# First two blocks' modulation columns by single-column matmuls, with the first x tile loaded first and the x tiles taken in turn

## The chip, the cores and the metric

The kernel runs on one core of one Trainium2 chip. The metric is the device time of one execution in microseconds (us); smaller is better. Engines are named as the profile names them: PE is TensorE (PEld its weight loads), DVE is VectorE, ACT is ScalarE, POOL is GpSimd, and SP is SyncE, whose queue issues all the transfers spoken of here.

## What is computed

A decoder layer on 2048 tokens of width 1024, cut to what the change touches:

```python
def hybrid_layer(x, c, positions, w_ada, b_ada, g_pre, w_in, ...):
    mod = jnp.einsum('bd,de->be', jax.nn.silu(c), w_ada) + b_ada
    shift, scale, gate = jnp.split(mod, 3, axis=-1)
    h = rmsnorm(x, g_pre) * (1.0 + scale[:, None, :]) + shift[:, None, :]
    proj = jnp.einsum('bsd,de->bse', h, w_in)
    gu, gv, gg, rq, rk, rv, rg = jnp.split(proj, PROJ_SPLITS, axis=-1)
    y_gmlp = gmlp_branch(gu, gv, gg, gmlp_ln_g, gmlp_ws, gmlp_bs)
    y_ret = retention_branch(rq, rk, rv, rg, positions, ret_gn_g)
    y = jnp.concatenate([y_gmlp, y_ret], axis=-1)
    y = rmsnorm(jnp.einsum('bsm,md->bsd', y, w_out), g_post)
    return x + gate[:, None, :] * y
```

## The kernel before

The 1024 channels are eight blocks of 128 (`kb` = 0 to 7). h is kept with the channels on the partitions, so scale and shift are one column each per block: `a_col[:, kb]` and `s_col[:, kb]`. Every large product is made of three f32r matmuls on high and low halves (`hh`, `hl` of h; `wh`, `wl` of the weights), 512 columns wide. The weights' halves are made on the way: `pump` takes the next weight block, ACT casts it to `wh` (L198), and another engine subtracts to get `wl` (L201).

The change lies in `start`, which handles the first 512 tokens (four tiles `xs[0]` to `xs[3]` of 128 tokens by 1024). For block 0 each tile goes through this chain:

- `stat(t)`: ACT squares and sums the tile (L283), POOL makes the reciprocal root of the mean in two operations (L286, L287);
- `scaled(t, a, b)`: DVE multiplies a range of the tile's columns by it (L933);
- `turn0(t)`: PE transposes the first 128 channels into PSUM (L922);
- `high0(t)`: ACT applies scale and shift and writes `hh` (L901); it needs `a_col` and `s_col` of block 0;
- `mms0(t)`: PE multiplies `hh` with the two weight halves (L929, L930).

`mod(kb)` makes the two columns of a block on DVE: for each it multiplies a slab of the modulation weights (`slab`, 128 by 1024, channels on the partitions) with `crow`, the row silu(c) spread to all partitions, and sums along the row (L897). `crow` is loaded ahead of all slabs and x tiles, and ACT applies silu to it (L879).

After the four tiles, `turn(1)` transposes block 1 of all four (L889), `qk_high(0)` makes two more products of block 0 (L977, L978), `h_low` on DVE makes `hl` of block 0 (L910, L912), and PE multiplies it (L1021, L1023). Then the loop over `kb` runs: in step `kb` PE multiplies block `kb` (L992, L993 and on) while ACT and DVE prepare block `kb + 1`: `hh` and `t` on ACT (both L901), `hl` on DVE (L912), then `mod(kb + 2)` on DVE and two `wl`. The stages after `start` (other tokens, rotary tables, retention, gMLP, the output product) are not touched.

What sets the order: on PE, ACT, DVE and POOL the instructions run in the order in which the program writes them, so an instruction that waits holds all that is written behind it on its engine. SP's queue issues transfers in its own order, and each waits until the buffer that it fills is free.

Of the kernel before, what the change touches and what calls it, by code (L numbers as in the profile page):

```python
# [11 lines left out]
F32 = mybir.dt.float32  # L12
# [3 lines left out]
AF = mybir.ActivationFunctionType  # L16
# [84 lines left out]
def tile_hybrid_layer(ctx: ExitStack, tc, x, xt, wm, wg, win, wun, wout, wst, cols, rows, pos, cst,  # L101
# [161 lines left out]
    def pump(eng=V, gap=1, ahead=3):  # L263
        if done[0] < len(worder):
            wsplit(worder[done[0]], eng, gap)
            done[0] += 1
        for i in worder[done[0]:done[0] + ahead]:
            wdma(i)
# [4 lines left out]
    def xload(pool, half, q, t, parts=1):  # L273
        row = half * HALF + q * QT + t * P
        xx = pool.tile([P, D], F32, name=f"xs{half}{q}{t}", tag="x", bufs=XBUF[half])
        for n in range(parts):
            cs = slice(n * D // parts, (n + 1) * D // parts)
            SP.dma_start(xx[:, cs], x[row:row + P, cs])
        return xx

    def xmean(xx, ss):
        jk = slot("jk", (xx.shape[-1],), BF16)
        S.activation(jk, xx, AF.Square, scale=1.0 / 32.0, accum_out=ss)  # L283
# [575 lines left out]
    def start(sp):  # L859
        def slab_load(kb):  # L860
            sl = [sp.tile([P, D], F32, name="slab", tag="x", bufs=XBUF[0]) for _ in range(2)]
            for t, n in zip(sl, range(2)):
                SP.dma_start(t, wm[kb, :, n, :])
            return sl

        crow = sp.tile([P, D], F32, name="crow")
        SP.dma_start(crow, rows[0:1, 2560:3584].partition_broadcast(P))
        slabs = {0: slab_load(0)}
        xs = [xload(sp, 0, 0, 0)]
        wdma(worder[0])  # L870
        xs += [xload(sp, 0, 0, t, 1 + t // 3) for t in range(1, QUAD)]
        wdma(worder[1])
        for n in (1, 2):
            slabs[n] = slab_load(n)
            for i in range(2):
                wdma(worder[2 * n + i])
        pv = [ps_m.tile([P, 512], F32, name=f"pv0{c}", tag="m") for c in range(QUAD)]
        pq0, pq1, tp = (ps_s.tile([P, 512], F32, name=n, tag="sm") for n in ("pq0", "pq1", "tp0"))
        S.activation(crow, crow, AF.Silu)  # L879
        xk, xn = {}, {}  # L880

        def xsums(tiles, ss, rs, ts):
            for t in ts:
                xmean(tiles[t], ss[:, t:t + 1])
                rsqrt_eps(rs[:, t:t + 1], ss[:, t:t + 1])

        def turn(kb):
            for c in range(QUAD):
                T.transpose(tp[:, c * P:(c + 1) * P], xs[c][:, kb * P:(kb + 1) * P], ident)  # L889
            xk[kb] = slot("xk")  # L890
            S.copy(xk[kb], tp)

        def mod(kb):
            for t, col, first, by in zip(slabs.pop(kb), (a_col, s_col), (b1g, cols_t[:, 8:16]),
                                         (cols_t[:, 24 + kb:25 + kb], 1.0)):
                jk = slot("jm", (D,), BF16)
                V.tensor_tensor_reduce(jk, t, crow, by, first[:, kb:kb + 1], ALU.mult, ALU.add,  # L897
                                       col[:, kb:kb + 1])

        def h_high(kb, src, hi):  # L900
            S.activation(hi, src, AF.Identity, bias=s_col[:, kb:kb + 1], scale=a_col[:, kb:kb + 1])  # L901

        def h_low(kb, parts, eng=V):
            hi, lo = hT[0, 0, kb]
            t = slot("t2")
            for cs, src in parts:
                if eng is S:
                    h_high(kb, src, t[:, cs])
                    continue
                V.tensor_scalar(t[:, cs], src, a_col[:, kb:kb + 1], s_col[:, kb:kb + 1], ALU.mult,  # L910
                                ALU.add)
            return lambda: V.tensor_tensor(lo, t, hi.bitcast(F32), ALU.subtract)  # L912

        ss = small.tile([P, QUAD + 1], F32, name="ss")
        rs = small.tile([P, QUAD], F32, name="rs")
        hi0 = hnew(0, 0, 0)[0]

        def t0(c):
            return (tp, pq1)[c % 2][:, c // 2 * P:(c // 2 + 1) * P]

        def turn0(c):
            T.transpose(t0(c), xs[c][:, 0:P], ident)  # L922

        def high0(c):
            h_high(0, t0(c), hi0[:, c * P:(c + 1) * P])

        def mms0(c):
            l, w = hchunk(0, c, 0), blocks[0]
            T.matmul(pv[c], l[0], w[0], start=True, stop=False)  # L929
            T.matmul(pv[c], l[0], w[1], start=False, stop=False)  # L930

        def scaled(t, a, b):
            V.tensor_scalar(xs[t][:, a:b], xs[t][:, a:b], rs[:, t:t + 1], None, ALU.mult)  # L933

        def stat(t):
            xmean(xs[t], ss[:, t:t + 1])
            rsqrt_eps(rs[:, t:t + 1], ss[:, t:t + 1])

        stat(0)
        pump(G, 0, 0)  # L940
        mod(0)
        scaled(0, 0, P)
        scaled(0, P, D)
        turn0(0)
        stat(1)
        high0(0)
        stat(2)
        scaled(1, 0, P)
        scaled(1, P, D)
        turn0(1)  # L950
        mms0(0)
        high0(1)
        xmean(xs[3][:, 0:512], ss[:, 3:4])
        scaled(2, 0, P)
        scaled(2, P, D)
        turn0(2)
        mms0(1)
        xmean(xs[3][:, 512:D], ss[:, 4:5])
        G.tensor_tensor(ss[:, 3:4], ss[:, 3:4], ss[:, 4:5], ALU.add)
        rsqrt_eps(rs[:, 3:4], ss[:, 3:4])  # L960
        high0(2)
        pump(G, 0, 0)
        scaled(3, 0, P)
        scaled(3, P, 2 * P)
        turn0(3)
        mms0(2)
        high0(3)
        mms0(3)
        low = h_low(0, [(slice(c * P, (c + 1) * P), t0(c)) for c in (0, 2, 1, 3)])
        low()  # L970
        mod(1)
        scaled(3, 2 * P, D)
        def qk_high(kb):
            w = blocks[KB + kb]
            for p, c in zip((pq0, pq1), range(2)):
                l = hchunk(0, c, kb)
                T.matmul(p, l[0], w[0], start=kb == 0, stop=False)  # L977
                T.matmul(p, l[0], w[1], start=False, stop=False)  # L978

        ss1 = small.tile([P, QUAD], F32, name="ss")  # L980
        rs1 = small.tile([P, QUAD], F32, name="rs")
        for kb in range(KB):
            f, e = kb == 0, kb == KB - 1
            if kb + 3 < KB:
                slabs[kb + 3] = slab_load(kb + 3)
                for i in range(2):
                    wdma(worder[2 * (kb + 3) + i])
            w, wq = blocks[kb], blocks[KB + kb]
            for c in range(QUAD):
                if not f:  # L990
                    l = hchunk(0, c, kb)
                    T.matmul(pv[c], l[0], w[0], start=False, stop=False)  # L992
                    T.matmul(pv[c], l[0], w[1], start=False, stop=False)  # L993
                if c == 1 and not e:
                    if kb == KB - 2:
                        xsums(xn, ss1, rs1, range(1))
                    turn(kb + 1)
                    pump(V, 0, 0)
                    pump(V, 0, 0)
            if f:  # L1000
                qk_high(kb)
            if not e:
                h_high(kb + 1, xk[kb + 1], hnew(0, 0, kb + 1)[0])
                low = h_low(kb + 1, [(slice(0, QT), xk[kb + 1])], S)
                low()
                if kb + 2 < KB:
                    mod(kb + 2)
            if kb == KB - 3:
                xn = [xload(sp, 0, 1, t) for t in range(QUAD)]
                SP.dma_start(wst_t, wst)  # L1010
                SP.dma_start(bs_b, rows[0:1, 0:512].rearrange("o (g t) -> o g t", g=4)
                             .partition_broadcast(P))
            if kb == KB - 2:
                G.tensor_tensor(wst_t, wst_t, mask.unsqueeze(1).broadcast_to([P, GROUPS, P]), ALU.mult)
                xsums(xn, ss1, rs1, range(1, 3))
            if e:
                xsums(xn, ss1, rs1, range(3, QUAD))
            if not f:
                qk_high(kb)
            for c in range(QUAD):  # L1020
                T.matmul(pv[c], hchunk(0, c, kb)[1], w[0], start=False, stop=e)  # L1021
            for p, c in zip((pq0, pq1), range(2)):
                T.matmul(p, hchunk(0, c, kb)[1], wq[0], start=False, stop=e)  # L1023
        return pv, (pq0, pq1), rs1
# [275 lines left out]
```

## Time and profile before

| | us |
|---|---|
| median of three runs | 882.3 (879.62 to 882.65) |
| the profiled execution's own time | 881.76 |
| its span in the trace | 880.0 |
| PE busy in the span | 845.7 |
| DVE busy | 673.3 |
| POOL busy | 358.1 |
| ACT busy | 313.0 |

The profiled execution lies 0.5 us under the median, and 1.76 us of its time lie outside the span. PE is busy for 96% of the span, so what is of interest are the stretches in which it is not, and they lie at the start (before the first block's matmuls run without a gap) and at the end. Times of single instructions are counted from the span's start.

### The profile page before, as it was taken

The page shows a single profiled execution, that of the slowest core. Times are in us where ns is not written, and L with a number is a line of the kernel's source. Part 1 is how long each engine was busy: PE and PEld are TensorE (multiplying, and loading weights), DVE is VectorE, ACT ScalarE, POOL GpSimd, SP SyncE. Part 2 cuts the span into 40 slices and gives each one's busy share as a digit, 9 for nine tenths or more (in the row PEclk, how much of TensorE's full clock was granted, in tenths as well). Part 3 has the DMA queues.
Part 4 walks back from the last instruction along what each step waited for, and adds up shares of the span by engine and source line. Part 5 has one row for each costly group of instructions (what it writes and reads, how often), then busy time and mean ns, then how long its engine had stood idle before and what let it go on. Part 6 is the DMA issues. An engine that isn't in the chain of part 4 may idle for free.

```text
span 880.0 us, 11841 instructions
## 1 busy us (share of the span) xinstructions
PE 845.7 (96%) x4074; PEld 696.3 (79%) x4074; DVE 673.3 (77%) x1275; ACT 313.0 (36%) x611; POOL 358.1 (41%) x403
## 2 busy tenths in 40 slices
PE   1999999999999999999999999999999999899996
PEld 0778888888888888888888888888888767688884
DVE  3989885665996768997786665897448898978885
ACT  4674223232363334431111221345343444333331
POOL 2031264345756236300443234675566000644551
PEclk9999999999999999999999999999999999999998
DMA  8971331310013424654222100011424854565422
GB/s 321 329 266 37 96 105 64 96 37 1 1 60 96 133 72 155 198 173 155 60 72 74 49 1 1 1 49 37 121 83 151 280 187 149 184 180 163 144 106 86
DMA packets 61884, 100.59 MB, mean 114 GB/s; under 512 B 5888, under 2 KB 22400, under 8 KB 61824
## 3 DMA queue, kind: packets, MB, share of 16 engines
q1 hardware_dynamic: 61824, 99.83, 34.6%
q8 instruction: 32, 0.52, 0.2%
q14 instruction: 28, 0.23, 0.1%
HBM read 83.03 MB, written 16.78 MB: 113 GB/s over the span
## 4 chain that ended last, share of the span: by engine, by line
PE 84%; DVE 6%; issue 3%; DMA 3%; ACT 2%; POOL 1%; SPq 0%; DVEq 0%; POOLq 0%; ACTq 0%
PE pqk L258 6%; PE pqk L256 6%; PE pqk L257 6%; PE pY L258 4%; PE pY L256 4%; PE pY L257 3%; PE pv L256 3%; PE pv L258 3%; PE pv L257 3%; PE prv L257 3%; PE prv L256 2%; PE pX L256 2%; PE prv L258 2%; PE pX L258 2%; PE pX L257 2%
## 5 line engine op out<-in xcount | busy, mean ns | idle before, releaser
L256 PE MATMUL pqk<-wh,hh 128*128 128x512 f32 x240 | 102.5, 427 | 0.0
L524 POOL TENSOR_TENSOR rA<-rA,rB 128x512 f32<-128x512 f32 x32 | 42.9, 1340 | 133.4 <-DVE rB L516 96.5
L258 PE MATMUL pqk<-wh,hl 128*128 128x512 f32 x240 | 94.7, 394 | 0.0
L257 PE MATMUL pqk<-wl,hh 128*128 128x512 f32 x240 | 93.8, 391 | 0.0
L538 ACT COPY qkT<-tp 128x512 f32<-128x512 f32 x32 | 18.8, 588 | 160.1 <-PE tp L529 160.1
L698 POOL TENSOR_SCALAR zrs<-zss 128x1 f32<-128x1 f32 x16 | 18.2, 1140 | 128.7 <-ACT jz L691 128.0
L201 DVE TENSOR_TENSOR wl<-wr,wh 128x512 fp32r<-128x512 f32 x62 | 63.0, 1030 | 0.2
L258 PEld LDWEIGHTS pqk<-wh,hl 128*128 128x128 f32 x240 | 45.0, 188 | 10.6
L256 PE MATMUL pv<-wh,hh 128*128 128x512 f32 x128 | 52.1, 407 | 0.0
L257 PEld LDWEIGHTS pqk<-wl,hh 128*128 128x128 f32 x240 | 45.5, 189 | 6.7 <-issue 0.2
L256 PEld LDWEIGHTS pqk<-wh,hh 128*128 128x128 f32 x240 | 45.4, 189 | 6.5 <-issue 0.2
L258 PE MATMUL pv<-wh,hl 128*128 128x512 f32 x128 | 50.1, 391 | 0.0
L257 PE MATMUL pv<-wl,hh 128*128 128x512 f32 x128 | 50.0, 390 | 0.0
L514 DVE TENSOR_TENSOR rA<-pqk,cos_t 128x512 f32<-128x512 f32 x28 | 19.3, 688 | 32.0 <-PE pqk L258 32.0
L201 DVE TENSOR_TENSOR wl<-ut,wh 128x512 fp32r<-128x512 f32 x48 | 42.9, 913 | 0.5 <-ACT wh L198 0.3
L582 DVE TENSOR_SCALAR yq<-o,gmv,grs 128x128 f32<-128x128 f32 x64 | 23.3, 405 | 23.9 <-POOL grs L575 23.9
L241 POOL TENSOR_TENSOR ut<-ur,ut 128x512 f32<-128x512 f32 x24 | 35.8, 1492 | 13.6 <-DVE yT L790 7.2
L461 ACT ACTIVATE vh<-pv,nbv,rsv 128x128 f32<-128x128 f32 x64 | 24.2, 457 | 47.4 <-POOL nbv L456 47.4
L256 PE MATMUL zY<-wh,yh 128*128 128x512 f32 x96 | 38.2, 398 | 2.2 <-DVE u L694 2.2
L198 ACT CAST wh<-ut 128x512 fp32r<-128x512 f32 x48 | 28.7, 621 | 31.7 <-POOL ut L241 31.7
L258 PE MATMUL zY<-wh,yl 128*128 128x512 f32 x96 | 38.3, 399 | 1.2 <-DVE yl L644 1.2
L790 POOL TENSOR_TENSOR yT<-yT,c 128x512 f32<-128x512 f32 x15 | 24.5, 1638 | 35.9 <-DVE c L810 25.8
(258 smaller groups left out, 2571.1 us busy)
## 6 DMA issues: line engine op xcount, KB each, us to landing
wr<-in_win SPq DMA_DIRECT2D x64, 256.0 KB, 3.9
ur<-in_wun SPq DMA_DIRECT2D x48, 256.0 KB, 3.5
slab<-in_wm SPq DMA_DIRECT2D x16, 512.0 KB, 6.2
ya<-yd SPq DMA_DIRECT2D x32, 256.0 KB, 3.8
xr<-in_x SPq DMA_DIRECT2D x16, 512.0 KB, 5.2
out<-xr SPq DMA_DIRECT2D x32, 256.0 KB, 2.8
or<-in_wout SPq DMA_DIRECT2D x28, 256.0 KB, 3.1
xt<-in_xt SPq DMA_DIRECT2D x24, 256.0 KB, 4.2
```

Source lines behind the costliest of these rows:

```text
L198: S.copy(hi, r)
L201: eng.tensor_tensor(lo, r, hi.bitcast(F32), ALU.subtract)
L241: G.tensor_tensor(r[name], r[a], r[b], ALU.subtract)
L256: T.matmul(ps, l[0], r[0], start=first, stop=False, skip_group_check=reopened)
L257: T.matmul(ps, l[0], r[1], start=False, stop=False, skip_group_check=reopened)
L258: T.matmul(ps, l[1], r[0], start=False, stop=last, skip_group_check=reopened)
L461: S.activation(vh[:, g, :], ps[:, g * P:(g + 1) * P], AF.Identity, bias=nb[:, g:g + 1], scale=rs[:, g:g + 1])
L514: V.tensor_tensor(A, ps.rearrange("p (g d) -> p g d", g=8), tab["cos"][:, ch, :].unsqueeze(1).broadcast_to([P, 8, 64]), ALU.mult)
L524: G.tensor_tensor(A, A, box["B"].rearrange("p g h d -> p (g h d)"), ALU.add)
L538: S.copy(qkT, box["tp"])
L582: V.tensor_scalar(yq[h][:, ch % QUAD, :], box["o"][:, i, :], mv[:, i, 0:1], rs[:, i:i + 1], ALU.subtract, ALU.mult)
L790: eng.tensor_tensor(y, y, by, ALU.mult)
```

## The change

Scale and shift of blocks 0 and 1 are made by `mod_pe` on PE, from slabs laid out with the contracted channels on the partitions (the host lays out these four slabs anew): eight f32 matmuls per column, each with 128x128 of the slab as the stationary operand and one column of silu(c), `sc`, as the moving one. Two small DVE operations then add the biases and the gain. `mod` on DVE stays for blocks 2 to 7. Since `crow` is then first needed for block 2, it is loaded later and its silu is moved into the loop. The first x tile is loaded ahead of all slabs. The statistics of the four x tiles are written in turn: a tile's statistics stand behind the `high0` of the tile before. The `wl` of the first two weight blocks move from POOL to DVE.

```diff
         crow = sp.tile([P, D], F32, name="crow")
+        xs = [xload(sp, 0, 0, 0)]
+        slabs = {0: slab_load(0)}
+        wdma(worder[0])
+        xs += [xload(sp, 0, 0, t) for t in range(1, QUAD)]
+        wdma(worder[1])
+        slabs[1] = slab_load(1)
+        for i in (2, 3):
+            wdma(worder[i])
         SP.dma_start(crow, rows[0:1, 2560:3584].partition_broadcast(P))
-        slabs = {0: slab_load(0)}
-        xs = [xload(sp, 0, 0, 0)]
-        wdma(worder[0])
-        xs += [xload(sp, 0, 0, t, 1 + t // 3) for t in range(1, QUAD)]
-        wdma(worder[1])
-        for n in (1, 2):
-            slabs[n] = slab_load(n)
-            for i in range(2):
-                wdma(worder[2 * n + i])
+        slabs[2] = slab_load(2)
+        for i in (4, 5):
+            wdma(worder[i])
...
+        pc = ps_s.tile([P, 512], F32, name="pc", tag="sm")
...
-        S.activation(crow, crow, AF.Silu)
...
+        def mod_pe(kb):
+            for n, t in enumerate(slabs.pop(kb)):
+                for k in range(KB):
+                    T.matmul(pc[:, 2 * kb + n:2 * kb + n + 1], t[:, k * P:(k + 1) * P], sc[:, k:k + 1],
+                             start=k == 0, stop=k == KB - 1)
+            V.scalar_tensor_tensor(a_col[:, kb:kb + 1], pc[:, 2 * kb:2 * kb + 1],
+                                   cols_t[:, 24 + kb:25 + kb], b1g[:, kb:kb + 1], ALU.mult, ALU.add)
+            V.tensor_tensor(s_col[:, kb:kb + 1], pc[:, 2 * kb + 1:2 * kb + 2],
+                            cols_t[:, 8 + kb:9 + kb], ALU.add)
...
         stat(0)
-        pump(G, 0, 0)
-        mod(0)
         scaled(0, 0, P)
+        mod_pe(0)
+        turn0(0)
+        pump(V, 0, 0)
         scaled(0, P, D)
-        turn0(0)
-        stat(1)
         high0(0)
-        stat(2)
...
+        for t in range(1, QUAD):
+            stat(t)
+            scaled(t, 0, P)
+            turn0(t)
+            high0(t)
+            mms0(t - 1)
+            scaled(t, P, D)
+        pump(V, 0, 0)
+        mms0(QUAD - 1)
         low = h_low(0, [(slice(c * P, (c + 1) * P), t0(c)) for c in (0, 2, 1, 3)])
         low()
-        mod(1)
-        scaled(3, 2 * P, D)
...
             if f:
                 qk_high(kb)
+                mod_pe(1)
             if not e:
                 h_high(kb + 1, xk[kb + 1], hnew(0, 0, kb + 1)[0])
                 low = h_low(kb + 1, [(slice(0, QT), xk[kb + 1])], S)
                 low()
+                if f:
+                    S.activation(crow, crow, AF.Silu)
```

On ACT at the start, before the change (`jk` rows are the statistics of a tile, `hh` rows are `high0`; `xs_104`, `108`, `110`, `112` are the four tiles):

```order
L879 ACTIVATE crow<-crow 128x1024
L283 ACTIVATE jk,ss<-xs_104 128x1024
L198 CAST wh<-wr 128x512
L283 ACTIVATE jk,ss<-xs_108 128x1024
L901 ACTIVATE hh<-tp_139,s_col,a_col 128x128
L283 ACTIVATE jk,ss<-xs_110 128x1024
L901 ACTIVATE hh<-pq_138,s_col,a_col 128x128
L283 ACTIVATE jk,ss<-xs_112 128x512 x2
L901 ACTIVATE hh<-tp_139,s_col,a_col 128x128
L198 CAST wh<-wr 128x512
L901 ACTIVATE hh<-pq_138,s_col,a_col 128x128
```

The same place on ACT after the change (the tiles are now `xs_99`, `107`, `109`, `111`):

```order
L283 ACTIVATE jk,ss<-xs_99 128x1024
L198 CAST wh<-wr 128x512
L913 ACTIVATE hh<-tp_138,s_col,a_col 128x128
L283 ACTIVATE jk,ss<-xs_107 128x1024
L913 ACTIVATE hh<-pq_137,s_col,a_col 128x128
L283 ACTIVATE jk,ss<-xs_109 128x1024
L913 ACTIVATE hh<-tp_138,s_col,a_col 128x128
L283 ACTIVATE jk,ss<-xs_111 128x1024
L913 ACTIVATE hh<-pq_137,s_col,a_col 128x128
L198 CAST wh<-wr 128x512
```

Before, the statistics of a tile stood ahead of the `hh` of the tile before; now they stand behind it.

On PE at the very start, before the change:

```order
L922 MATMUL tp_139<-cst_t,xs_104 128x128
L922 MATMUL pq_138<-cst_t,xs_108 128x128
L929 MATMUL pv_133<-wh,hh 128x512
L930 MATMUL pv_133<-wl,hh 128x512
L922 MATMUL tp_139<-cst_t,xs_110 128x128
```

The same place on PE after it (`pc` holds the columns in PSUM):

```order
L905 MATMUL pc<-sc,slab 128x1 x16
L934 MATMUL tp_138<-cst_t,xs_99 128x128
L934 MATMUL pq_137<-cst_t,xs_107 128x128
L941 MATMUL pv_132<-wh,hh 128x512
L942 MATMUL pv_132<-wl,hh 128x512
L934 MATMUL tp_138<-cst_t,xs_109 128x128
```

The sixteen single-column matmuls of block 0 now stand ahead of the first transpose.

On PE behind the fourth tile, before the change (`turn(1)`, `qk_high(0)`, then the products with `hl`):

```order
L889 MATMUL tp_139<-cst_t,xs_112 128x128
L977 MATMUL pq_137<-wh,hh 128x512
L978 MATMUL pq_137<-wl,hh 128x512
L977 MATMUL pq_138<-wh,hh 128x512
L978 MATMUL pq_138<-wl,hh 128x512
L1021 MATMUL pv_133<-wh,hl 128x512
```

The same place on PE after it:

```order
L891 MATMUL tp_138<-cst_t,xs_111 128x128
L974 MATMUL pq_136<-wh,hh 128x512
L975 MATMUL pq_136<-wl,hh 128x512
L974 MATMUL pq_137<-wh,hh 128x512
L975 MATMUL pq_137<-wl,hh 128x512
L905 MATMUL pc<-sc,slab 128x1 x16
L1021 MATMUL pv_132<-wh,hl 128x512
```

The sixteen single-column matmuls of block 1 now stand between `qk_high(0)` and the products with `hl`.

## Rows read from the trace of the kernel before

**Rows 1.** Page, parts 1 and 2: busy time by engine; granted clock in 40 slices

```profile
PE 845.7 (96%) x4074; PEld 696.3 (79%) x4074; DVE 673.3 (77%) x1275; ACT 313.0 (36%) x611; POOL 358.1 (41%) x403
PEclk9999999999999999999999999999999999999998
```

**Rows 2.** Stretches: length, busy PE, PEld, DVE, ACT, POOL, clock, DMA share, GB/s

```profile
26.79:60.00 33.21, 32.93 (x149) 25.47 (x150) 29.29 (x47) 23.74 (x39) 5.33 (x8) 1.00 0.92 319
60.00:200.00 140.00, 139.50 (x765) 117.74 (x764) 104.86 (x240) 43.48 (x88) 55.17 (x87) 1.00 0.23 73
```

**Rows 3.** Timeline of ACT: start, length, operation, [idle before, releaser]

```profile
6.68 1.06 ACT L879 ACTIVATE crow<-crow 128x1024 f32<-128x1024 f32 x1 [4.10 <-DMA crow<-in_rows]
11.10 1.06 ACT L283 ACTIVATE jk<-xs 128x1024 bf16<-128x1024 f32 x1 [3.36 <-DMA xs<-in_x]
...
15.05 0.46 ACT L901 ACTIVATE hh<-tp,s_col,a_col 128x128 fp32r<-128x128 f32 x1 [0.86 <-PE tp L922]
15.41 1.04 ACT L283 ACTIVATE jk<-xs 128x1024 bf16<-128x1024 f32 x1
...
18.35 0.46 ACT L901 ACTIVATE hh<-tp,s_col,a_col 128x128 fp32r<-128x128 f32 x1
18.71 0.61 ACT L198 CAST wh<-wr 128x512 fp32r<-128x512 f32 x1
21.40 0.46 ACT L901 ACTIVATE hh<-pq,s_col,a_col 128x128 fp32r<-128x128 f32 x1 [2.08 <-PE pq L922]
...
25.92 0.82 ACT L901 ACTIVATE hh<-xk,s_col,a_col 128x512 fp32r<-128x512 f32 x1 [0.28 <-DVE s_col L897]
```

**Rows 4.** Timeline of POOL, behind the third tile's statistics

```profile
16.91 0.55 POOL L287 TENSOR_TENSOR rs<-rs,nhalf 128x1 f32<-128x1 f32 x1
```

**Rows 5.** Timeline of DVE, first 29 us

```profile
3.52 0.16 DVE L130 SCALAR_TENSOR_TENSOR b1g<-cols_t 128x8 f32<-128x8 f32 x1
8.71 1.34 DVE L897 CUSTOM_DVE_ANT_0 jm<-slab,crow,b1g 128x1024 bf16<-128x1024 f32 x1 [5.03 <-DMA slab<-in_wm]
...
9.97 1.28 DVE L897 CUSTOM_DVE_ANT_0 jm<-slab,crow,cols_t 128x1024 bf16<-128x1024 f32 x1
...
17.49 0.88 DVE L933 TENSOR_SCALAR xs<-xs,rs 128x128 f32<-128x128 f32 x2 [0.81 <-POOL rs L287]
...
20.95 0.72 DVE L910 TENSOR_SCALAR t<-tp,a_col,s_col 128x128 f32<-128x128 f32 x2
...
26.27 1.29 DVE L201 TENSOR_TENSOR wl<-wr,wh 128x512 fp32r<-128x512 f32 x2
27.48 0.69 DVE L912 TENSOR_TENSOR hl<-t,hh 128x512 fp32r<-128x512 f32 x1
28.09 1.34 DVE L897 CUSTOM_DVE_ANT_0 jm<-slab,crow,b1g 128x1024 bf16<-128x1024 f32 x1
```

**Rows 6.** Timeline of PE: third tile's transpose, block 1's transposes, `qk_high(0)`, first `hl` products

```profile
17.84 0.48 PE L922 MATMUL tp<-cst_t,xs 128*128 128x128 f32 x1 [0.36 <-DVE xs L933]
...
22.93 1.04 PE L889 MATMUL tp<-cst_t,xs 128*128 128x128 f32 x4
23.64 0.56 PE L977 MATMUL pq<-wh,hh 128*128 128x512 f32 x1
...
24.74 1.08 PE L1021 MATMUL pv<-wh,hl 128*128 128x512 f32 x4
```

**Rows 7.** Timeline of PE's weight loads at the start

```profile
16.42 0.33 PEld L930 LDWEIGHTS pv<-wl,hh 128*128 128x128 f32 x1
...
22.93 0.65 PEld L889 LDWEIGHTS tp<-cst_t,xs 128*128 128x128 f32 x3 [0.20 <-issue]
```

**Rows 8.** Groups by shape, matmuls, then weight loads, of L467: count, busy us, mean ns

```profile
L467 PE MATMUL mx<-wst_t,vh 128*128 128x128 f32 x128 | 16.8, 274 | 0.0
...
L467 PEld LDWEIGHTS mx<-wst_t,vh 128*128 128x128 f32 x128 | 16.7, 191 | 1.3
```

**Rows 9.** Timeline of PE, one chunk's L467 matmuls in the full flow

```profile
214.05 1.05 PE L467 MATMUL mx<-wst_t,vh 128*128 128x128 f32 x8
```

More of the change, by code (lines that the diff above doesn't have):

```diff
@@ L939, in start @@
         stat(0)
-        pump(G, 0, 0)
-        mod(0)
         scaled(0, 0, P)
+        mod_pe(0)
+        turn0(0)
+        pump(V, 0, 0)
         scaled(0, P, D)
-        turn0(0)
-        stat(1)
         high0(0)
-        stat(2)
[L948 to L968, printed above, removed]
+        for t in range(1, QUAD):
[7 more added lines that the diff above has]
+        mms0(QUAD - 1)
         low = h_low(0, [(slice(c * P, (c + 1) * P), t0(c)) for c in (0, 2, 1, 3)])
         low()
-        mod(1)
-        scaled(3, 2 * P, D)
         def qk_high(kb):
@@ L1254 @@
     wm = np.stack([wa[1], wa[0]], axis=2)
+    for kb in range(2):
+        for n in range(2):
+            wm[kb, :, n, :] = w_ada[:, (1 - n) * D + kb * P:(1 - n) * D + (kb + 1) * P].reshape(
+                KB, P, P).transpose(1, 0, 2).reshape(P, D)
     wg = w_ada[:, 2 * D:].reshape(KB, P, D)
```

## The prediction

> **What bounds the kernel now.** I read the page first: PE is busy 845.7 of 880.0 us [rows 1], so 34.3 us are left. The stretches say where they are not: from 26.79 to 60 PE is busy 32.93 of 33.21 us, from 60 to 200 it is busy 139.50 of 140 [rows 2]. More than half of the gap lies at the start: the statistics of the first tile begin at 11.10, and its `hh`, without which PE has no product, at 15.05 [rows 3]. Everything behind the start runs on PE without slack, so I take a shift of the point where block 1's flow begins to the end one for one. That point I measure by ACT's `hh` of block 1, at 25.92 [rows 3]; PE's first product of block 1 follows it.
>
> How 25.92 comes about, by ACT's timeline: x tile 0 has landed at 11.10, behind `crow` (6.68) and the slabs. Of the four `high0` the first begins at 15.05, the third at 18.35 and the last at 21.40 [rows 3], 6.35 after the first. From there to 25.92 are 4.52 us, and `hh` of block 1 waited for `s_col` from DVE [rows 3], which is `mod(1)`.
>
> **First term: the four tiles in turn.** The order rows show each tile's statistics behind the `hh` of the tile before. The trace has this very loop once: `hh` of tile 0 at 15.05, right behind it the squares of tile 2 at 15.41, POOL's power at 16.91 [rows 4], DVE's scaling at 17.49 [rows 5], PE's transpose at 17.84 [rows 6], `hh` of tile 2 at 18.35 [rows 3]. That is 3.30 us, each step starting when the one before ends. Before, two such loops ran interleaved; now there is one. Three rounds make 9.90 us from the first to the last `high0`, against 6.35: +3.55. PE at its higher clock would save some 0.2 in a round, which I leave to the range. The tile order takes something away from this: the later tiles land earlier than before by one 512 KB transfer (`crow`, behind them now), but they have landed long before ACT asks.
>
> **Second term: when the first `high0` can start.** It needs the transpose of tile 0 and both columns of block 0. Tile 0 takes `crow`'s place in the queue, so it lands at about 6.68 [rows 3] in place of 11.10. That gain of 4.4 us is worth nothing if the columns are later. The slabs keep their places behind one 512 KB transfer: the first has landed at 8.71, the second by 9.97, where DVE read it without a wait [rows 5]. Behind them, `mod` took DVE two operations. Now PE runs sixteen f32 matmuls, and the trace says what one f32 matmul is: L467 is called 64 times (16 chunks of four groups) and has 128 records with 128 weight loads [rows 8]. So a call is two passes, each with a load of its own, and a `mod_pe` is 32 passes.
>
> The price of a pass with one moving column stands nowhere in the trace; a weight load for it does. Eight passes of L467 take 1.05 us with the last one 0.27 [rows 8, 9], so (1.05 - 0.27) / 7 = 0.11 us from pass to pass in the full flow, load included. At the start PE is slower: there a load takes 0.33 us [rows 7] against 0.19 [rows 8], and three loads in a row take 0.65, 0.22 each [rows 7]. The granted clock is printed as full in those slices [rows 1], so I go by the durations and call the two levels 1.2 and 2.4 GHz. Bounds for a pass: 0 below (all of it might hide), 0.33 above (loads that don't overlap at the lower level). PE has done nothing before 8.71, so I take the lower level for all of block 0, at twice 0.11, 0.21: 32 x 0.21 = 6.7, which ends at 15.4. The last pass's own tail (0.2) and two small DVE operations like L130's 0.16 [rows 5] add 0.55: the first `high0` starts at 16.0, against 15.05: +0.95. The transpose of tile 0 stands behind the 32 passes on PE and is ready at about 15.9, so it hides.
>
> The Trainium skill, "TensorE: Matmul & The Clock Gate", section "LDWEIGHTS (loading the stationary operand)", gives a load of 128 columns as 128 / 1.2 ns, 107 ns, with no second figure for another clock. The 0.11 of the full flow agrees; the longer loads of rows 7 speak against one figure for both levels. By it the time is that of the second rival below.
>
> With both terms the last `high0` starts at 16.0 + 9.9 = 25.9, against 21.40: +4.5.
>
> **Third term: from the last `high0` to block 1.** Before, 4.52 us. Now, in order: `hh`'s share 0.36 (18.35 to 18.71 [rows 3]), the cast 0.61 [rows 3], its `wl`, which has moved from POOL to DVE ahead of the reads of the transposes, 0.65 (half of 1.29 [rows 5]), those reads of the first bank 0.72 [rows 5]: 2.4 with the hops. Only then may `turn(1)` overwrite that bank: 1.04 [rows 6]. `qk_high(0)` takes 1.10 (23.64 to 24.74 [rows 6]): 4.55. Then the 32 passes of block 1; PE has worked without pause by then and I take 0.11: 3.5. With 0.55 for the tail and DVE, `hh` of block 1 starts 8.6 us behind the last `high0`: +4.1. `mod(1)`, 2.6 us of DVE, is saved, but it no longer ends last. The slabs of block 1 come one transfer earlier than before and wait for PE by then.
>
> **Fourth term: `crow`.** Its silu (1.06 [rows 3]) now stands behind block 1's second activation on ACT, and `mod(2)` waits for it. Before, `mod(2)` started 0.61 behind the start of `hl` (27.48 to 28.09 [rows 5]), which itself started as that activation ended. So it starts 1.06 behind it now, +0.45, and the loop carries that on.
>
> POOL loses two subtractions and one add, which nobody waits for. The DVE work for the small columns is in the sums. The later slabs wait for PE's reads in place of DVE's: the slabs whose buffers `mod_pe(1)` frees are for blocks 3 and 4, which DVE comes to only after `mod(2)`, so they hide as before; if not, the loop would pay a landing once.
>
> **Sum.** 0.95 + 3.55 + 4.1 + 0.45 = 9.05 us. On the profiled execution's 881.76 that is **890.8 us**; the median of the runs lies 0.5 above that execution, which is within the noise of the sum.
>
> **Rivals.** *Cheap passes, no slower than before.* If a single-column pass cost nothing, the first `high0` would start at 9.97 + 0.55 = 10.5, the last at 20.4, `hh` of block 1 at 20.4 + 4.55 + 0.55 = 25.5 against 25.92, and with `crow` the time is 881.8: a tie. Each 0.01 us of a pass adds 0.48 (the second slab's 16 and block 1's 32; the first slab's hide behind the second's landing), so up to about 0.09 the change stays inside 0.5%. For it: only one column moves. Against it: every pass has its own load [rows 8]. The time at half that bound is 884.0. The Trainium skill, "TensorE: Matmul & The Clock Gate", section "Wait — 56ns, not 53.3ns?", gives 25 ns as the least distance between matmuls however small; by that the sum would be 1.2 us over the tie.
>
> *Loads at 0.11 from the start.* If the level doesn't matter to a load, or PE rises to the higher one during block 0's passes, these end at 8.71 + 3.5 = 12.2, the first `high0` starts at 12.8, and the sum is 3.2 less: 887.6. For it: 32 passes in a row keep PE at work. Against it: the 0.33 and 0.22 of rows 7.
>
> *PE stays at the lower level.* If columns of width one don't hold the higher clock, block 1's passes take 0.21 too, +3.2, and the first products of block 1 start slow, as `qk_high`'s first did (0.56 [rows 6]); some 1.5 us more. That gives 895.5. With loads that don't overlap at either level (0.33, then 0.19) it is 32 x 0.12 + 32 x 0.08 = 6.4 over the sum: 897.2.
>
> **How the numbers follow.** Forecast, about 890.8: 0.50. Loads at 0.11 throughout, 887.6: 0.20. Lower level kept, 895.5: 0.12, and loads that don't overlap, 897.2: 0.04. Cheap passes, 881.8 to 886: 0.14. The range reaches from 885.5, inside the cheap case, to 897, and leaves out some 0.16. A measurement tells about 0.5% from no change, 877.9 to 886.7. Slower by more: 0.50 + 0.12 + 0.04 and most of the 0.20, 0.83. Within it: 0.15. Faster: 0.02, since even passes for nothing only tie; it would take slabs that land some 5 us earlier.
>
> **What would show it.** Right: `high0` at about 16, 19.3, 22.6 and 25.9, with ACT idle between each tile's statistics and its `hh`; 64 weight loads for `pc`, the first ones 0.2 apart and the later ones 0.11; `hh` of block 1 near 34.5; from there on the same flow as before, 9 us later. Wrong: rounds clearly under 3.3, loads under 0.1 apart in block 0, or `hh` of block 1 before 30.

## The result, and the profile after

The changed kernel takes 894.66 us (median of four executions, 890.29 to 897.16) against 882.17 us (879.62 to 882.65): a ratio of 1.0142, with a 95% interval of 1.0097 to 1.0187. It is slower by 12.5 us, where 9 were forecast. The profiled execution took 893.83 us. Its page, with the span, the busy time of each engine and the granted clock in 40 slices, answers to [rows 1]:

```profile
span 892.1 us, 11959 instructions
...
PE 859.9 (96%) x4138; PEld 711.6 (80%) x4138; DVE 669.9 (75%) x1272; ACT 311.4 (35%) x609; POOL 355.1 (40%) x400
...
PEclk9999999999999999999999999999999999999998
```

The span has grown by 12.1 us, PE's busy time by 14.2, and what PE doesn't work has shrunk from 34.3 to 32.2. ACT, DVE and POOL have less to do than before. The balance doesn't say by itself where the time went: block 0's passes count as busy time of PE, and they stand where PE waited before. The timelines do. Behind the start PE has still no slack (stretches in the columns of [rows 2]; the first ends where `hh` of block 1 is about to start):

```profile
26.79:36.00 9.21, 8.56 (x37) 7.86 (x36) 3.54 (x8) 1.62 (x3) 0.00 (x0) 1.00 0.14 42
36.00:60.00 24.00, 24.00 (x102) 19.78 (x103) 17.93 (x30) 14.73 (x23) 0.00 (x0) 1.00 0.72 241
60.00:200.00 140.00, 139.53 (x752) 117.13 (x752) 108.00 (x235) 51.45 (x101) 53.00 (x81) 1.00 0.33 103
```

In the first stretch PE is busy 8.56 of 9.21 us while ACT works 1.62, so ACT waits for PE. ACT's timeline shows it row by row (start, length, operation, idle before it and what ended it), as [rows 3] did before:

```profile
5.42 1.06 ACT L283 ACTIVATE jk<-xs 128x1024 bf16<-128x1024 f32 x1 [2.73 <-DMA xs<-in_x]
...
15.48 0.46 ACT L913 ACTIVATE hh<-tp,s_col,a_col 128x128 fp32r<-128x128 f32 x1 [4.95 <-DVE s_col L909]
15.84 1.05 ACT L283 ACTIVATE jk<-xs 128x1024 bf16<-128x1024 f32 x1
18.79 0.46 ACT L913 ACTIVATE hh<-pq,s_col,a_col 128x128 fp32r<-128x128 f32 x1 [1.81 <-PE pq L934]
...
22.08 0.46 ACT L913 ACTIVATE hh<-tp,s_col,a_col 128x128 fp32r<-128x128 f32 x1 [1.80 <-PE tp L934]
...
25.37 0.46 ACT L913 ACTIVATE hh<-pq,s_col,a_col 128x128 fp32r<-128x128 f32 x1 [1.80 <-PE pq L934]
...
37.62 0.81 ACT L913 ACTIVATE hh<-xk,s_col,a_col 128x512 fp32r<-128x512 f32 x1 [7.08 <-DVE s_col L909]
...
42.56 0.59 ACT L893 COPY xk<-tp 128x512 f32<-128x512 f32 x1 [2.48 <-PE tp L891]
43.05 1.15 ACT L198 CAST wh<-wr 128x512 fp32r<-128x512 f32 x2
44.09 0.81 ACT L913 ACTIVATE hh<-xk,s_col,a_col 128x512 fp32r<-128x512 f32 x1
```

Three places stand out. The first `high0` waits 4.95 us for the columns although tile 0 has been there since 5.42. Each later `high0` waits 1.8 us for its tile's own transpose. And `hh` of block 1, at 37.62, waits 7.08 us for `s_col`; before, it stood at 25.92 and waited 0.28.

PE's timeline has what they wait for (`pc` are the passes of `mod_pe`, L974 and L975 `qk_high(0)`, L1021 the products with `hl`, L990 those of block 1):

```profile
8.10 6.96 PE L905 MATMUL pc<-sc,slab 128*128 128x1 f32 x32 [8.10 <-DMA slab<-in_wm]
...
18.27 0.47 PE L934 MATMUL pq<-cst_t,xs 128*128 128x128 f32 x1 [2.90 <-DVE xs L945]
...
27.76 1.11 PE L891 MATMUL tp<-cst_t,xs 128*128 128x128 f32 x4 [0.65 <-DVE t L922]
28.53 0.78 PE L974 MATMUL pq<-wh,hh 128*128 128x512 f32 x1
...
29.95 0.63 PE L975 MATMUL pq<-wl,hh 128*128 128x512 f32 x1
30.38 6.82 PE L905 MATMUL pc<-sc,slab 128*128 128x1 f32 x32
37.06 2.05 PE L1021 MATMUL pv<-wh,hl 128*128 128x512 f32 x4
...
42.75 0.55 PE L990 MATMUL pv<-wl,hh 128*128 128x512 f32 x1
43.14 0.40 PE L989 MATMUL pv<-wh,hh 128*128 128x512 f32 x1
```

A `mod_pe` is 32 passes, as forecast, and takes 6.96 us for block 0 and 6.82 for block 1. With a last pass of 0.35 that is (6.96 - 0.35) / 31 = 0.21 us from pass to pass, in both. The same lower level shows in the products: 0.63 a product at 29.95, 2.05 for four at 37.06 (1.08 before [rows 6]), and only from 43.14 on the 0.40 of the full flow. By the durations PE runs at the lower level from its first instruction to some 43 us, with pauses of 2.90, 1.96, 1.96 and 0.65 us up to 27.76 and none after that. The printed clock is 1.00 all the way in this trace, so here the durations tell and not that column.

The chain of work that ended last, in its first 48 us, has both groups of passes whole, each in one piece:

```profile
8.10 6.97 PE pc L905 x32
...
30.58 6.62 PE pc L905 x32
```

### The profile page after: what moved, and what is told of

Same layout as the page of the kernel before. It is cut to its first block, busy times and chain, and to the rows that moved or that the text cites. A ratio compares the mean times of both kernels' runs of the same rounds, so it can differ in the third digit from the quotient of the medians.

```text
span 892.1 us, 11959 instructions
## 1 busy us (share of the span) xinstructions
PE 859.9 (96%) x4138; PEld 711.6 (80%) x4138; DVE 669.9 (75%) x1272; ACT 311.4 (35%) x609; POOL 355.1 (40%) x400
## 4 chain that ended last, share of the span: by engine, by line
PE 88%; DVE 5%; DMA 3%; issue 2%; ACT 1%; POOL 1%; SPq 0%; DVEq 0%; POOLq 0%; ACTq 0%
PE pqk L258 6%; PE pqk L256 6%; PE pqk L257 6%; PE pY L258 3%; PE pY L256 3%; PE pY L257 3%; PE pv L258 3%; PE pv L256 3%; PE pv L257 3%; PE prv L257 2%; PE prv L256 2%; PE prv L258 2%; PE pX L257 2%; PE pX L258 2%; PE pX L256 2%; PE pZ L257 2%
## 5 line engine op out<-in xcount | busy, mean ns | idle before, releaser
L201 DVE TENSOR_TENSOR wl<-wr,wh 128x512 fp32r<-128x512 f32 x64 | 65.4, 1034 | 3.1 <-ACT wh L198 3.0
L198 ACT CAST wh<-wr 128x512 fp32r<-128x512 f32 x64 | 37.4, 617 | 5.3 <-DMA wr<-in_win 5.3
```

Of the source, the lines that this page charges most:

```text
L198: S.copy(hi, r)
L201: eng.tensor_tensor(lo, r, hi.bitcast(F32), ALU.subtract)
```

## The experiments

The theory: three separate costs stand one behind the other on the way to block 2: the tiles in turn, block 1's passes on PE, and a PE that stays at the lower level. The rivals: that one of them explains all of it, that a pass hides behind something else, or that the lower level is an accident of the start that work on PE cures. Each kernel below ran beside the kernel before (median 881.9 for the first four, 881.71 for the others, 882.17 beside the changed kernel); differences between two of them can be off by that 0.5 us.

| kernel | first `high0` | last `high0` | `hh` block 1 | `hh` block 2 | median against before, us |
|---|---|---|---|---|---|
| before | 15.05 | 21.40 | 25.92 | 30.74 | 0 |
| after | 15.48 | 25.37 | 37.62 | 44.09 | +12.5 |
| block 1's columns on DVE | 15.61 | 26.45 | 32.71 | 37.52 | +7.8 |
| statistics one tile ahead | 15.58 | 20.74 | 32.98 | 39.45 | +7.1 |
| PE kept busy at the start | 13.54 | 23.44 | 35.68 | 40.99 | +10.2 |
| block 0's passes twice | 22.67 | 32.56 | 44.81 | 51.28 | +18.6 |
| before, tiles in turn | 14.79 | 24.69 | 30.12 | 34.93 | +5.6 |
| before, x tile first | 14.63 | 21.01 | 25.53 | 30.34 | -1.6 |
| all three cures | 12.79 | 18.47 | 24.73 | 29.54 | -0.9 |
| two cures, PE not kept busy | 15.50 | 20.66 | 26.93 | 31.74 | +1.1 |

The middle columns are starts in us on ACT's timeline of the profiled execution. The shift at block 2 is what comes out at the end, within 2 us either way, in every line. So a shift of the start does go to the end one for one, as the prediction took it. Most of what is left between the traces has a cause that they show. In five of them (before, block 1's columns on DVE, PE kept busy, x tile first, all three cures) the granted clock falls near 770 us to the lower level for 3.4 us; in the other five it does not. From `hh` of block 2 to the end the five with the fall take 849.2 to 850.5 us, the five without it 848.0 to 848.8. The same place before and after (columns of [rows 2]):

```profile
764.50:768.00 3.50, 3.50 (x10) 2.76 (x9) 2.89 (x5) 0.00 (x0) 0.00 (x0) 0.51 1.02 375
```
```profile
776.50:780.00 3.50, 2.68 (x12) 2.24 (x13) 3.50 (x6) 0.40 (x1) 1.28 (x1) 1.00 1.00 382
```

Twelve 512-wide products there take 4.41 us before (from 763.72) and 2.83 after (from 777.32), and in both PE had waited 2.17 us just ahead of them. Why the level fell in one and not in the other stays open; the change doesn't touch this stage.

### Block 1's columns back on DVE

```diff
+        SP.dma_start(crow, rows[0:1, 2560:3584].partition_broadcast(P))
         slabs[1] = slab_load(1)
...
-        SP.dma_start(crow, rows[0:1, 2560:3584].partition_broadcast(P))
...
             scaled(t, P, D)
+            if t == 2:
+                S.activation(crow, crow, AF.Silu)
...
         low()
+        mod(1)
...
                 qk_high(kb)
-                mod_pe(1)
...
-                if f:
-                    S.activation(crow, crow, AF.Silu)
```

The host lays out only the slabs of block 0 anew here.

> The changed kernel with the columns of block 1 back on DVE (mod(1), with crow loaded ahead of block 1's slabs and its silu on ACT between the third and fourth tile). Theory, that block 1's 32 passes on PE at the lower clock level stand on the path: hh of block 1 starts some 5 us behind the last high0 in place of 12.25, PE rises to the higher level about 6 us sooner, and the time falls by 7 to 8.5 us, to about 886.5. Rival, that the time went into the tiles' turns and the columns of block 0 alone, and block 1's wait only shows a delay that something else would have caused (the loads, or DVE): the time falls by under 2 us.

Measured: 889.74 us (ratio 1.0088, 1.0073 to 1.0103), 4.9 under the changed kernel, 6.6 at block 2. That is less than the 7 to 8.5 that were expected, and far more than the rival's 2. Of the 6.6 some 1.6 are lost near 770 us, where this trace has the fall of the clock and that of the changed kernel has not. From this kernel's timeline ACT's rows around the last `high0`, then PE's first products with `hl`:

```profile
22.56 1.05 ACT L966 ACTIVATE crow<-crow 128x1024 f32<-128x1024 f32 x1
...
26.45 0.46 ACT L913 ACTIVATE hh<-pq,s_col,a_col 128x128 fp32r<-128x128 f32 x1 [1.80 <-PE pq L934]
...
32.71 0.81 ACT L913 ACTIVATE hh<-xk,s_col,a_col 128x512 fp32r<-128x512 f32 x1 [1.10 <-DVE s_col L899]
```
```profile
31.45 1.21 PE L1021 MATMUL pv<-wh,hl 128*128 128x512 f32 x4
```

`hh` of block 1 stands 6.26 us behind the last `high0` in place of 12.25 (some 5 expected). So the passes are no free ride: with `mod(1)` on DVE the same step is 6 us shorter. I lost one of them again by putting `crow`'s silu into the third round, which made the last round 4.24 us. And without the passes PE rises sooner: four L1021 take 1.21 us here, 2.05 there.

### Statistics one tile ahead

```diff
+        stat(1)
         high0(0)
         for t in range(1, QUAD):
-            stat(t)
+            if t + 1 < QUAD:
+                stat(t + 1)
             scaled(t, 0, P)
```

> The changed kernel with each tile's statistics written ahead of the high0 of the tile before, as in the kernel before. Theory, that the single loop of 3.30 us a tile costs 3.5 us or more: the last high0 starts at 20.5 to 22 in place of 25.37, and the time falls by 3.5 to 5 us, to about 890. Rival, that the tiles' turns hide behind something later (block 1's columns, which wait for slabs or for PE anyway): hh of block 1 stays near 37.6 and the time stays within 1 us.

Measured: 888.96 us (1.0077, 1.0056 to 1.0099), 5.7 under the changed kernel; 4.6 in the trace at both blocks (3.5 to 5 us were expected). Four `high0` now span 5.16 us, less than the 6.35 of before, so writing the statistics ahead takes away all that the turns had added. On PE's timeline block 1's passes are as long as ever:

```profile
25.75 6.82 PE L905 MATMUL pc<-sc,slab 128*128 128x1 f32 x32
```

### PE kept busy from the start

```diff
+        wide = sp.tile([P, 512], BF16, name="wide")
+        G.memset(wide, 1.0)
...
+        for _ in range(18):
+            T.matmul(pv[3], wide[:, 0:P], wide, start=True, stop=True)
         stat(0)
         scaled(0, 0, P)
         mod_pe(0)
```

> The changed kernel with 18 extra matmuls of 512 columns (bf16, on a tile of ones; their result is overwritten) on PE ahead of the first columns, in the time in which PE waits for the first slab. Theory, that a single-column pass costs one weight load and the load goes by PE's level: if PE comes to the passes at the higher level, they are 0.11 apart in place of 0.21, block 0's 32 take 3.5 us in place of 6.96, the first high0 starts near 12.1 in place of 15.48, and the time falls by some 3.4 us. If PE falls back to the lower level during the passes, the gain is between 0 and 3.4 and the trace shows at which pass. Rival, that a pass costs 0.21 at either level (issue, or a read that doesn't overlap): they stay 0.21 apart and the time does not fall.

Measured: 892.13 us (1.0109, 1.0088 to 1.0129), 2.5 under the changed kernel. The intervals of the two ratios overlap, so it is the trace that shows the gain: 1.94 us at the first `high0` and at block 1, 3.10 at block 2. The 18 products are of no use but to keep PE at work. PE's timeline (whole, then from windows that begin and end inside the passes), and stretches of the passes alone (length, busy PE, PEld, DVE with counts, granted clock, DMA share, GB/s; a pass counts in each stretch that it touches):

```profile
1.33 6.97 PE L954 MATMUL pv<-wide 128*128 128x512 bf16 x18 [1.33 <-POOL wide L867]
8.31 4.81 PE L907 MATMUL pc<-sc,slab 128*128 128x1 f32 x32
```
```profile
8.31 2.48 PE L907 MATMUL pc<-sc,slab 128*128 128x1 f32 x21
...
10.84 2.27 PE L907 MATMUL pc<-sc,slab 128*128 128x1 f32 x10
```
```profile
8.30:9.30 1.00, 0.99 (x9) 1.00 (x10) 0.00 (x0) 1.00 1.05 422
9.30:10.30 1.00, 1.00 (x11) 1.00 (x11) 0.00 (x0) 1.00 1.03 420
10.30:11.30 1.00, 1.00 (x9) 1.00 (x8) 0.00 (x0) 0.69 1.04 426
11.30:12.30 1.00, 1.00 (x6) 1.00 (x7) 0.00 (x0) 0.50 1.00 406
12.30:13.30 1.00, 0.82 (x4) 0.73 (x4) 0.14 (x2) 0.50 1.02 399
```

Here the clock column does speak. At a granted clock of 1.00 (2.4 GHz) the first 21 passes are (2.48 - 0.25) / 20 = 0.11 us apart; at 0.50 (1.2 GHz) the last ten are (2.27 - 0.35) / 9 = 0.21 apart, where 0.25 and 0.35 are the lengths of a last pass. So the price goes with the level, and the rival of 0.21 at either level is out. The clock falls from the one to the other, at the 22nd pass, while passes follow one another without a gap: in this execution these matmuls fill PE's busy row, yet the higher level is not kept while they run. A warm start is thus worth 2.1 us for block 0's passes and not the 3.3 of the full step. Block 1's 32 passes take 6.82 us here as well, and block 2 follows block 1 after 5.31 us, not 6.47: PE rises 5 us earlier on this trace, at 37.8.

### Block 0's passes twice

```diff
             for n, t in enumerate(slabs.pop(kb)):
-                for k in range(KB):
+                for again in range(2 if kb == 0 else 1):
+                    for k in range(KB):
```

> The changed kernel with the sixteen single-column matmuls of block 0 run twice (the second run of each group of eight overwrites the first). Theory, that the 32 passes stand whole on the path: another 32 x 0.214 = 6.85 us between the first slab and the first high0, which moves from 15.48 to 22.3, and the time rises by about 6.9 us to about 901. Rival, that the start is set by the loads and the tiles' statistics and the passes are partly hidden: it rises by clearly less than 5.

Measured: 900.53 us (1.0211, 1.0194 to 1.0228), 5.9 over the changed kernel, and 7.2 in the trace at each of the columns of the table. The passes of block 0 on PE's timeline:

```profile
8.46 13.78 PE L906 MATMUL pc<-sc,slab 128*128 128x1 f32 x64 [8.46 <-DMA slab<-in_wm]
```

32 more passes are 6.82 us more, 0.213 each, and nothing hides one; the other 0.36 of the 7.2 is the first slab, which landed that much later. PE stayed at the lower level through 13.78 us of passes without a gap: the second 32 take as long as the first.

### The kernel before, with the tiles in turn only

```diff
-        stat(1)
         high0(0)
-        stat(2)
-        scaled(1, 0, P)
...
+        for t in range(1, QUAD):
+            stat(t)
+            scaled(t, 0, P)
+            turn0(t)
+            high0(t)
+            mms0(t - 1)
+            scaled(t, P, D)
```

> The kernel before (columns of all blocks on DVE, loads in its order) with one part of the change alone: the tiles' statistics written in turn, a tile's behind the high0 of the tile before. Theory, that the single loop of 3.30 us a tile is a cost of its own, whatever makes the columns: the high0 start at about 14.8, 18.1, 21.4 and 24.7 against 15.05 to 21.40, block 1's hh starts 3 to 3.5 us later than 25.92, and the time rises by about 3.3 us (0.4%). Rival, that it hides behind mod(1) and block 1's loads: the time stays within 1 us.

Measured: 887.27 us (1.0059, 1.004 to 1.0078), +5.6 in the median and +4.2 in the trace at both blocks. The turns alone thus make the kernel slower, with `mod` still on DVE. (The fourth tile's statistics, in two halves before, are one piece here, as in the changed kernel.) First to last `high0` is 9.90 us, to the hundredth what was forecast, and the last `high0` is 3.3 later than before. Most of the rest of the 4.2 goes with an accident of this edit: a `wl` on POOL falls on `hl`, which takes 1.53 us where it takes 0.69 in [rows 5]. DVE's row and then POOL's:

```profile
26.02 1.53 DVE L912 TENSOR_TENSOR hl<-t,hh 128x512 fp32r<-128x512 f32 x1
```
```profile
25.73 1.27 POOL L201 TENSOR_TENSOR wl<-wr,wh 128x512 fp32r<-128x512 f32 x1 [1.93 <-ACT wh L198]
```

### The kernel before, with the first x tile first only

```diff
         crow = sp.tile([P, D], F32, name="crow")
+        xs = [xload(sp, 0, 0, 0)]
         SP.dma_start(crow, rows[0:1, 2560:3584].partition_broadcast(P))
         slabs = {0: slab_load(0)}
-        xs = [xload(sp, 0, 0, 0)]
```

> The kernel before with another part alone: the first x tile is loaded ahead of crow and the slabs, all else as it was. Theory, that the earlier landing is worth little, since the statistics of the second tile (on ACT ahead of the first high0) wait for their tile as before and crow and the slabs land one transfer later: x tile 0 lands at 5.4 to 6.7, the first high0 starts 0.5 to 1.5 us sooner, the last within 1 us of 21.40, and the time changes by less than 1 us. Rival, that the landing at 11.1 bounds the start: the last high0 and the time come 2 to 4 us sooner.

Measured: 880.11 us (0.9984, 0.9974 to 0.9994), -1.6 in the median and -0.4 in the trace. Under 1 us was expected, and 0.5 to 1.5 at the first `high0`, which gains 0.42; the profiled execution, at 882.46, is the slowest of the twelve. That `mod` on DVE needs `crow` limits what it can give, as ACT's timeline and then DVE's show:

```profile
7.53 1.06 ACT L879 ACTIVATE crow<-crow 128x1024 f32<-128x1024 f32 x1 [4.95 <-DMA crow<-in_rows]
8.49 1.04 ACT L283 ACTIVATE jk<-xs 128x1024 bf16<-128x1024 f32 x1
```
```profile
10.23 1.34 DVE L897 CUSTOM_DVE_ANT_0 jm<-slab,crow,b1g 128x1024 bf16<-128x1024 f32 x1 [6.25 <-DMA slab<-in_wm]
```

The statistics of tile 0 start 2.6 us earlier than before, the first slab is read 1.5 us later, and the gain at the first `high0` stays small. This part of the change harms nothing.

### The cures together

This kernel is the changed one with the first three edits above (`mod(1)` on DVE, statistics one tile ahead, PE kept busy); a second one leaves the last of them out:

```diff
+        for _ in range(18):
+            T.matmul(pv[3], wide[:, 0:P], wide, start=True, stop=True)
...
+        stat(1)
...
-            stat(t)
+            if t + 1 < QUAD:
+                stat(t + 1)
...
+        mod(1)
...
-                mod_pe(1)
```

The memset of `wide` and the moves of `crow` and its silu are as above and not shown again.

> The changed kernel with three of its costs taken out at once: block 1's columns on DVE, the statistics written ahead, and the 18 extra matmuls ahead of block 0's passes (their result is overwritten). Theory: first high0 near 13.5, last near 18.5 to 19, block 1's hh at 23.5 to 25 against 25.92, so the time is 1 to 2.5 us under the kernel before, about 880, which this measurement can hardly tell from no change. Rival, that the start of block 1 has another bound (block 1's slabs, which land at 17 to 19, and DVE's order behind hl): hh of block 1 at 26 or later and the time no better than before.

> As the one with three costs out, without the extra matmuls: block 1's columns on DVE and the statistics ahead, block 0's passes at the lower level. Theory, that the three costs add: first high0 at 15.5, last at 20.7, block 1's hh near 26 to 27, the time within 1 us of the kernel before and 1.5 to 2 us over the one with the extra matmuls.

Measured: 880.8 us (0.9992, 0.998 to 1.0004) with all three, and 882.79 us (1.0018, 1.0006 to 1.0031) without the busy PE (within 1 us of before was expected, 1.1 came). The two cures alone bring back 11.4 of the 12.5 us, each against the kernel before beside it. What they leave of the change (block 0's columns on PE, the x tile first and the new order of the loads, two `wl` on DVE) costs about a microsecond in sum; its parts were not taken apart further. With all three, block 0's passes run on PE's timeline as

```profile
8.64 3.70 PE L907 MATMUL pc<-sc,slab 128*128 128x1 f32 x32 [0.77 <-DMA slab<-in_wm]
```

that is 0.11 us each, all at the higher level, and in the trace 1.2 us are gained at block 1. In the median 0.9 are, which is not to be told from nothing. PE's stretches here (length, busy PE, granted clock, DMA share, GB/s) show the fall behind the passes and not in them:

```profile
11.60:12.40 0.80, 0.80 (x8) 1.00 1.05 425
...
13.40:15.00 1.60, 0.35 (x2) 0.50 1.03 407
```

So the same 32 passes after the same 18 products lost the level at the 22nd pass in one execution and kept it to their end in the other. When it falls is not settled by these runs. A rise during passes was never seen: in all four traces with block 1's passes on PE, PE comes to them at the lower level and they take 6.82 us.

## Why the prediction was right, and where it was short

The direction came out as predicted, and so did the mechanism of the two large terms: the tiles in turn, and passes that nothing hides. The level that PE has in block 1's passes did not, and `crow` did not reach the path. The forecast of 890.8 us is 3.9 under the median. The sum on the profiled execution, by its four terms:

| term | forecast | measured |
|---|---|---|
| first `high0` | +0.95 | +0.43 |
| first to last `high0` | +3.55 | +3.54 |
| last `high0` to block 1 | +4.1 | +7.73 |
| block 1 to block 2 | +0.45 | +1.65 |
| sum | +9.05 | +13.35 |

From block 2 to the end of the span 1.25 us of this are gained again (12.1). That is not the change's doing: the trace of before has the fall of the clock at 764.5 us, which costs it about 1.6, and that of the changed kernel has none.

**The tiles in turn** (first term of the text). Right. The three rounds took 3.31, 3.29 and 3.29 us, from one loop that [rows 3 to 6] held for one tile. The kernel before with this edit alone repeats the 9.90, and with the statistics one tile ahead it is 5.16.

**The first `high0`.** Right, and 0.5 us too high, since the first slab landed at 8.10 and not at 8.71. The price of a pass, 0.21 at the lower level, was taken from L467's 0.11 at the higher one [rows 8, 9] and the three loads of [rows 7], and it held to the hundredth. The view of one tile's instructions (duration min, median, max; first and last start) has the 64 loads that were to be seen:

```profile
L905 PEld LDWEIGHTS pc<-sc,slab x64: 288/333/333, 8.1 to 36.8; 128*128 128x128 f32 x64
L905 PE MATMUL pc<-sc,slab x64: 205/352/353, 8.1 to 36.8; 128*128 128x1 f32 x64
```

333 ns of a load, 0.21 us apart: the records of the loads overlap. At the higher level passes with one moving column (0.11, all three cures) cost as much as L467's with 128 [rows 9], so between these two the width of the moving operand doesn't set the price. That it is the load which does is argued from this. The Trainium skill, "TensorE: Matmul & The Clock Gate", section "LDWEIGHTS (loading the stationary operand)", gives P / 1.2 ns for P columns, 107 ns for 128, and no second figure for another level. The 3.70 us above agree with it at the higher level; the 6.82 and 6.96 don't. That also settles the rival with cheap passes: 0.21 is far above the 0.09 at which it began to hold.

**From the last `high0` to block 1.** Here is the step that failed: "PE has worked without pause by then and I take 0.11". It took 0.21, for 32 passes 3.3 us more, and the premise didn't hold either: PE had waited 2.90, 1.96, 1.96 and 0.65 us between its pieces. Of what was to be seen, loads 0.11 apart in block 1 and `hh` of block 1 near 34.5, neither came (0.21 and 37.62). The parts before the passes came out as forecast in their order (2.39 us to `turn(1)`, 2.4 forecast), but `turn(1)` and `qk_high(0)` took 2.62 and not 2.15, at the same lower level. (The 2.15 itself is too long for before: it adds 1.04 and 1.10, which overlap; from 22.93 to 24.74 [rows 6] are 1.81.) Before, PE had risen by 24.74 [rows 6], and I carried that over to a start in which PE works in short pieces with 2 to 3 us of waiting between them. The first rows of `after` at that place, 0.78 and 0.63 a product, show that it had not risen by 30.38; then came 6.82 us of passes, all of them at the lower level.

**`crow`.** This term did not reach the path. DVE starts `mod(2)` 0.95 us behind the start of `hl` in place of 0.61, where 1.06 was forecast. But it has written `s_col` of block 2 at 42.59 (DVE's timeline), 1.5 us before `hh` of that block starts:

```profile
42.59 0.08 DVE L899 DVE_READ_ACCUMULATOR2_ANT s_col<- 128x1 f32 x1
```

ACT's rows of the changed kernel show what this `hh` stands behind: two casts, and these behind the copy of `turn(2)`, which waited 2.48 us for PE, whose products were still at the lower level. With PE kept busy, PE rose sooner and the wait is shorter, but it is the same wait (ACT's timeline there):

```profile
37.11 1.04 ACT L1009 ACTIVATE crow<-crow 128x1024 f32<-128x1024 f32 x1
39.47 0.59 ACT L895 COPY xk<-tp 128x512 f32<-128x512 f32 x1 [1.32 <-PE tp L893]
```

ACT was done with the silu there and idle for 1.32 us. Block 2 came after 5.31 us, 0.5 more than the 4.82 of before. So all of the 1.65 is a wait for PE: 1.2 of it went with the earlier rise, and the other 0.5 also stands behind PE's transposes. That it is near the 0.45 forecast for `crow` is chance.

**The rivals.** The one that happened is the third, a PE that stays at the lower level, at 895.5 with a chance of 0.12. Its terms, 3.2 for the passes and 1.5 for slow first products, measured 3.3 and 2.1 (0.47 + 1.65), while the 0.45 for `crow` fell away. In one point it differs too: PE didn't fall from the higher level; it had not yet risen when block 1's passes began. I had the row that spoke for it, `qk_high`'s first product at 0.56, and named the condition ("if columns of width one don't hold the higher clock"), but gave more weight to a PE that is busy. The Trainium skill, "TensorE: Matmul & The Clock Gate", section "What's actually happening", says that the default state is throttled and that activity releases the throttle. The 13.78 us of passes at a constant 0.21 are a full busy row in which no such release came; the reason given for 0.11, that PE is busy by then, didn't hold here.

**What stays open.** When PE rises and falls differs between executions of similar kernels (37.8 in one, 2.6 us behind block 1's passes; some 43 in the other, 5.8 behind them). It may be why the changed kernel's times spread over 6.9 us and those of before over 3.0 (4.4 in the 29 executions beside the later kernels), but only the profiled execution has a trace, so that is not shown. The `wl` that moved from POOL to DVE, 0.69 us ahead of the reads of the transposes, was not tested apart. Passes for block 1 that start on a PE already at the higher level were not tried.

## What to carry to other kernels

A matrix-vector product on PE is priced by its passes, two for each f32 matmul of 128 by 128 and each with a weight load, at the level that PE has in that place; one moving column in place of 128 didn't make a pass cheaper here (0.11 us each at the higher level), and on a chain that everything waits for it has to beat the engine that it relieves. Take the level from durations of neighbouring instructions in the same stretch. In these traces PE's busy row was full during one-column passes and the level never rose in them; of two groups of passes that began at the higher level, one lost it on the way. Where an in-order engine serves several tiles, write the next tile's first step ahead of the instruction that waits: here that alone was worth 4.6 us in the trace.

## What the runs showed of the hardware that was not expected

- PE's busy row can be full (1.00 of 1.00 us) as its granted clock falls from 1.00 to 0.50, while the work is weight loads with one moving column each. In another execution the level was the lower one through 13.78 us of them.
- The granted clock is printed as 1.00 from the start of the traces of before and after, although products take 0.63 us there and 0.40 later. It was seen to read 0.50 in traces in which the clock had risen and fallen.
- In the place in the queue where the broadcast row `crow` had landed at 6.68 us, an x tile of the same 512 KB landed at 5.42.
- Near 770 us the granted clock fell to 0.50 for 3.4 us in five of ten traces, and twelve 512-wide products took 4.41 us in place of 2.83. PE had waited 2.17 us just ahead of them both in the trace of before, with the fall, and in that of the changed kernel, without it.
- `hl` on DVE took 1.53 us in place of 0.69 while POOL subtracted a `wl` (1.27 us).
